# Handing out weight buffers and chaining the first loads at the beginning of an MLP

## The chip, the cores and the metric

The kernel runs on one core of a Trainium2 chip. Its time is the device time of one execution in microseconds (us); where several executions were timed, the median stands with the lowest and the highest. A core has TensorE for matrix products (PE in the profile), VectorE (DVE), ScalarE (ACT), GpSimd (POOL) and SyncE (SP). Each runs its own instructions in the order of its own queue, and they wait for each other by semaphores. DMAs are issued by SP and by POOL here and run beside the engines.

## The reference, cut to what matters

The kernel computes two layers of a decoder trunk on a sequence of 512 tokens, width 1024, in float32. Each layer is a mixer (attention and an mLSTM branch, merged and projected), and then the MLP at whose beginning the change lies:

```python
    x = x + mixed @ w_out

    u = jax.nn.relu(rmsnorm(x, norm_ffn) @ w_ff1)
    return x + (u * u) @ w_ff2
```

`w_ff1` is 1024 x 4096 and `w_ff2` 4096 x 1024, for each layer.

## The kernel before, in words

Every float32 product is made of three TensorE products: both factors are split into a high part, which ACT rounds, and a low part, the difference, which DVE forms. `two_parts` does that (lines 1212 and 1213), and `mm3` (line 47 stands for its matmuls) multiplies high by high, high by low and low by high.

The MLP is cut into four parts of 1024 hidden columns. In each part the first product (512 tokens x 1024 by 1024 x 1024) and the second one are done as 2 x 2 blocks with seven block products instead of eight, numbered 1 to 7, each on a sum or a difference of blocks. One block product is a slot; `first_slots` gives those of the first product of a part (`f0`, `f1` for the parts 0 and 1), `second_slots` those of the second one (`p`). A slot has two halves `h`, each with a weight tile of 512 KB (128 x 1024 float32). A half of a first slot is 24 matmuls with 256 columns moving, a half of a second slot 12 matmuls with 512 columns.

The list `slots` is the order of the work: f0[2], f1[2], f0[1], f0[5], p[1], f0[6], f0[7], f0[4], f0[3], f1[1] and so on. For each half the kernel first prepares (`prep`: ask for the weights, split them, then call `then`, which can ask for more) and later runs it; preparing is four halves ahead in the program. The pool `spl` holds four pairs of split weights, so the fifth split waits until TensorE is done with the first pair.

The weights lie in eleven raw buffers, numbered 0 to 10. `raw` (line 1227) hands out the first free number of the list `idle_raws`, and `drop` gives a number back at the end of the list, once the tile's splits are in the program. The buffers lie over memory that the mixer before has used, in four groups: 0 and 1 ("b"), 2 ("d"), 4 to 6 ("c"), and 3 and 7 to 10 ("a"); a group comes free when the mixer's last reader of that memory is done. `ask` (line 1236) issues a load on SP (line 1239); each of the first loads is ordered behind the one before it, and from the fifth on the scheduler places them as it likes.

What a slot needs, with the names of the tiles in the instruction order of layer 0 (of which the last number stays from here on):

- f0[2]: block (0,1) of part 0, loads 3703 and 3709. f1[2]: block (0,1) of part 1, loads 3715 and then, for the second half, 3727.
- f0[1]: block (0,0), loads 3779 and 3830.
- f0[5], f0[6], f0[3]: the sum blocks `s`. `begin` (line 1389 for part 0) loads a block into `c` (3721, 3733), another into `s` (3723, 3735), adds them on DVE (`plus`, line 1249) and lets POOL add a third block to `c` by an accumulating DMA (`more`, line 1348). After f0[5] has split `s`, POOL adds one more block to it for f0[6], and then another for f0[3].
- f0[7]: the blocks `c`. p[1]: blocks of `w_ff2`, loads 3958 and 3992. f0[4]: block (1,1), loads 4138 and 4173. The sum blocks of part 1: loads 4144 and 4179, each with an accumulating DMA behind it.

`begin0` is called in the prep of f1[2], so the sum blocks of part 0 take their buffers between the two halves of f1[2]; `begin1` is called in the prep of f0[4].

Beside the first five halves run the steps of the norm: for each of four column blocks `turn_whole` transposes x on TensorE into a bank of a pool of two (line 52), makes a high part on ACT (line 180) and a low part on DVE (line 181) for f0[1], and two scaled copies on ACT (line 1298). `t1` forms their difference on DVE, which ACT and DVE then split; it is the moving operand of f0[5]. `t2` does the same for f0[6]. After slot f0[2] ACT copies its bank to SBUF (line 1445), and so after f1[2], f0[5] and f0[6]; f0[7] adds to the bank that the copy after f0[6] reads.

Of the kernel before, what the change touches and what calls it, by code (L numbers as in the profile page):

```python
# [33 lines left out]
def hybrid_kernel(ctx, tc, x, norm_mix, w_in, att_q_norm, att_k_norm, att_sinks, m_gate_bias,  # L34
# [27 lines left out]
    def nm(s):  # L62
        uid[0] += 1
        return f"{s}_{uid[0]}"
# [4 lines left out]
    def pool(phase, name, bufs):  # L69
        now[name] = phase.enter_context(tc.tile_pool(name=name, bufs=bufs, reuse_waits="tile"))  # L70
        return now[name]
# [1114 lines left out]
    def mlp(l, norm, phase):  # L1186
# [6 lines left out]
        comb = pool(phase, "comb", 1)  # L1193
        uspl = pool(phase, "uspl", 2)
        spl = pool(phase, "spl", 4)
        raws, idle_raws = {}, list(range(11))
        for which, tags in (("a", (3, 7, 8, 9, 10)), ("b", (0, 1)), ("c", (4, 5, 6)), ("d", (2,))):
            raws.update(dict.fromkeys(tags, pool(phase, "raws_" + which, 1)))
        acts, ms = norm.acts, []
# [27 lines left out]
        def raw(shape):  # L1227

            n = idle_raws.pop(0)
            r = raws[n].tile(list(shape), F32, tag=f"r{n}", name=nm("raw"))  # L1230
            raw_place[id(r)] = (n, r)
            return r

        first_asked = []

        def ask(r, src):

            with tc.issue_after(first_asked[-1].ins) if first_asked else ExitStack():
                d = nc.sync.dma_start(r, src)  # L1239
            if len(first_asked) < 4:  # L1240
                first_asked.append(d)

        def drop(*gone):
# [3 lines left out]
        def plus(d, p, q, op=ALU.add):  # L1247
            with tc.high_priority():
                ve.tensor_tensor(d, p, q, op=op)
# [76 lines left out]
            t_parts[4] = two_parts(d, *t_new("t4"))  # L1326
            drop(d)

        def first_slots(part, new, places={}, begins=()):

# [2 lines left out]
            a11, a12, a22, s, c = ([None] * 2 for _ in range(5))  # L1335

            def src(h, i, j):
                c0 = 1024 * part + T * i + H * h
                return w_ff1[l, T * j:T * (j + 1), c0:c0 + H].rearrange("(k p) n -> p k n", p=P)

            def load(to, h, i, j):
                with tc.high_priority():
                    to[h] = raw([P, 4, H])
                    ask(to[h], src(h, i, j))

            def more(to, h, i, j):
                with tc.high_priority():
                    gp.dma_start(to[h], src(h, i, j), accum_op=ALU.add)  # L1348

            def w2(h):  # L1350
                load(a12, h, 0, 1)
                return a12[h], lambda: [f(h) for f in begins], a12[h]

            def begin(h):
                load(s, h, 1, 0)
                more(s, h, 1, 1)

            def w1(h):
                load(a11, h, 0, 0)
                return a11[h], lambda: begin(h) if part > 1 else None, a11[h]  # L1360

            def w5(h):
                def then():
                    more(s, h, 0, 0)
                    load(c, h, 0, 0)
                    more(c, h, 1, 0)

                return s[h], then
# [9 lines left out]

            def w4(h):
                load(a22, h, 1, 1)  # L1380
                return a22[h], lambda: [f(h) for f in begins] if part == 0 else None, a22[h]

            if part == 0:

                def begin(h):
                    load(c, h, 1, 0)
                    load(s, h, 1, 1)
                    plus(s[h], s[h], c[h])
                    more(c, h, 0, 0)

                def w2(h):
                    load(a12, h, 0, 1)
                    return a12[h], lambda: None, a12[h]

                def w5(h):
                    return s[h], lambda: more(s, h, 0, 0)
# [74 lines left out]
            else:  # L1471
                done1, done2 = lambda: then_read((0, 0), False, ALU.add), lambda: first_read((0, 0), True)

            return begin, {
                1: product_(1, False, True, w1, lambda: quad(0, 0), done1),
                2: product_(2, True, not seeded, w2, lambda: quad(1, 0), done2),
                5: product_(5, True, True, w5, lambda: t_parts[1], lambda: first_read((1, 1), True, -1.0)),
                6: product_(6, False, False, w6, lambda: t_parts[2], lambda: first_read((1, 0), False)),
                7: product_(7, False, False, w7, lambda: t_parts[3], lambda: then_read((1, 1), False, ALU.subtract)),
                4: product_(4, False, False, w4, lambda: t_parts[4], lambda: only_read((0, 1), False, -1.0)),  # L1480
                3: product_(3, True, False, w3, lambda: quad(1, 1), lambda: then_read((1, 0), True, ALU.add)),
            }
# [40 lines left out]
        def second_slots(part, u):  # L1523
# [9 lines left out]
            def load(to, h, i, j):  # L1533
                with tc.high_priority():
                    to[h] = raw([P, 2, T])
                    ask(to[h], src(h, i, j))
# [83 lines left out]


        us = [{key: quads.tile([P, 4, H], F32, tag=t, name=nm("u")) for key, t in buf[0].items()}, {}, {}, {}]
        f1s = []
        begin0, f0 = first_slots(0, us[0], {2: "y", 5: "y"}, [lambda h: f1s[0](h)])
        begin1, f1 = first_slots(1, us[1], {2: "x"}, [begin0])
        f1s.append(begin1)
        p = second_slots(0, us[0])
        slots = [f0[2], f1[2], f0[1], f0[5], p[1], f0[6], f0[7], f0[4], f0[3],
                 f1[1], p[5], f1[5], p[6], f1[6], p[3], f1[7], p[7], f1[3], p[4], f1[4], p[2]]
        for part in range(1, 4):  # L1630
            p = second_slots(part, us[part])
            if part < 3:
                f = first_slots(part + 1, us[part + 1])[1]
                slots += [p[1], f[1], p[2], f[2], p[5], f[5], p[6], f[6], p[3], f[7], p[7], f[3], p[4], f[4]]
            else:
                slots += [p[n] for n in (1, 5, 2, 6, 3, 7, 4)]
# [46 lines left out]
    for l in range(DEPTH):  # L1683
        with start if l == 0 else ExitStack() as phase:
            if l > 0:
                psum_pools(phase, 3)
            norm = mixer(l, norm, late, order, phase)
        with ExitStack() as phase:
            psum_pools(phase, 2)
            norm = mlp(l, norm, phase)  # L1690
        late = norm.steps(0, 1.5, 0.5, lambda k, norm=norm: turn_behind(norm, k)) if norm else []
        order = [4, 5, 6, 7, 0, 1, 2, 3]
# [40 lines left out]
```

## Time and profile before

| | |
|---|---|
| three timed executions | median 1309.32 us (1307.10 to 1311.42) |
| the profiled execution's own time | 1310.44 us |
| its span, from the first to the last instruction | 1308.7 us |
| TensorE busy | 1268.4 us, 97% |
| beginning of the MLP of layer 0, 322 to 337 us | TensorE busy for 6.71 of 15.00 us |
| mean granted clock of TensorE | 0.990 |

The profile shows one execution. In its groups and timelines a row has the engine, the line, the operation, what is written from what (without buffer numbers), the shape, the count and, in brackets, how long the engine stood idle before it and which work ended that. Times in a timeline are us from the start of the span. The lines of the timelines that matter are shown with the prediction.

### The profile page before, as it was taken

How to read it: one execution, taken by the hardware profiler on the slowest of the kernel's cores; microseconds unless marked ns; L12 is line 12 of the kernel's file. 1: busy time of each engine (PE TensorE's matmuls, PEld its weight loads, DVE VectorE, ACT ScalarE, POOL GpSimd, SP SyncE). 2: the span in 40 equal slices, each digit the busy share in tenths (PEclk: the TensorE clock that was granted, in tenths of full speed). 3: DMA queues.
4: the chain of work that ended last, by engine and by line, in shares of the span. 5: the costliest groups of instructions: out<-in, count | busy, mean ns of one | idle time of the engine just before them, and what ended most of it. 6: DMA issues, size and time to landing. Idle time of an engine off the chain costs nothing.

```text
span 1308.7 us, 19864 instructions
## 1 busy us (share of the span) xinstructions
PE 1268.4 (97%) x7170; PEld 1106.3 (85%) x7170; DVE 1027.8 (79%) x1620; ACT 818.1 (63%) x1435; POOL 289.2 (22%) x377
## 2 busy tenths in 40 slices
PE   9999999999699999999999999999996999999998
PEld 7887888888588989999888887888876988999987
DVE  5788987687668886878857989876876688778787
ACT  6578587645656665656554885875465556566563
POOL 4514131030213012131215132310303130211300
PEclk9999999999899999999999999999997999999999
DMA  5425463485998879897224345545859997899953
GB/s 158 114 68 150 106 114 113 133 163 147 193 228 150 224 184 212 218 192 210 34 72 113 108 112 114 111 121 128 170 155 190 227 170 206 185 210 228 193 145 97
DMA packets 147379, 201.78 MB, mean 154 GB/s; under 512 B 10825, under 2 KB 87473, under 8 KB 147281
## 3 DMA queue, kind: packets, MB, share of 16 engines
q0 software_dynamic: 52544, 70.39, 33.6%
q1 hardware_dynamic: 94016, 129.72, 32.5%
q8 instruction: 56, 0.92, 0.3%
q10 hardware_dynamic: 720, 0.40, 0.1%
q14 instruction: 43, 0.34, 0.1%
HBM read 197.33 MB, written 2.10 MB: 152 GB/s over the span
## 4 chain that ended last, share of the span: by engine, by line
PE 82%; DVE 6%; DMA 4%; ACT 3%; issue 2%; POOL 1%; SPq 0%; DVEq 0%; ACTq 0%; POOLq 0%
PE mm L47 70%; PE aux L47 11%; DMA raw<-in_w_ff_dram 4%; DVE wl L1213 2%; PE aux L52 2%; ACT t L664 1%; ACT wh L1212 1%; DMA w<-in_w_in_dram 1%; DVE wl L168 1%; DVE tq L625 0%; DVE p L748 0%; SPq L1239 0%; ACT u L1445 0%; POOL rp L547 0%; POOL rq L548 0%
## 5 line engine op out<-in xcount | busy, mean ns | idle before, releaser
L1213 DVE TENSOR_TENSOR wl<-raw,wh 128x1024 fp32r<-128x1024 f32 x224 | 270.9, 1220 | 118.5 <-ACT wh L1212 117.5
L47 PE MATMUL mm<-i,wh 128*128 128x256 f32 (+1 forms) x1344 | 336.8, 342 | 22.0 <-ACT wh L1212 18.1
L1212 ACT ACTIVATE wh<-raw 128x1024 fp32r<-128x1024 f32 x224 | 235.0, 1054 | 179.1 <-PE mm L47 88.7
L47 PEld LDWEIGHTS mm<-i,wh 128*128 128x128 f32 x1344 | 227.5, 193 | 43.0 <-ACT wh L1212 19.1
L47 PE MATMUL mm<-i,wl 128*128 128x256 f32 (+1 forms) x672 | 225.7, 337 | 0.0
L47 PE MATMUL mm<-wh,uh 128*128 128x512 f32 x440 | 172.7, 392 | 0.2 <-ACT uh L1212 0.2
L47 PE MATMUL mm<-wl,uh 128*128 128x512 f32 x440 | 172.1, 391 | 0.0
L47 PE MATMUL mm<-wh,ul 128*128 128x512 f32 x440 | 171.5, 390 | 0.0
L1348 POOL DMA_DIRECT2D raw<-in_w_ff_dram x60 | 77.5, 1315 | 407.0 <-DVE wl L1213 114.8
L47 PEld LDWEIGHTS mm<-i,wl 128*128 128x128 f32 x672 | 129.0, 192 | 13.4
L168 DVE TENSOR_TENSOR wl<-w,wh 128x512 fp32r<-128x512 f32 (+1 forms) x144 | 96.4, 673 | 37.2 <-ACT wh L167 36.2
L167 ACT ACTIVATE wh<-w 128x512 fp32r<-128x512 f32 (+1 forms) x144 | 86.4, 603 | 62.4 <-PE mm L47 43.9
L47 PE MATMUL mm<-t,wh 128*128 128x256 f32 x576 | 106.6, 287 | 5.9 <-ACT wh L1212 5.9
L47 PE MATMUL mm<-wh,i 128*128 128x512 f32 (+1 forms) x352 | 99.7, 357 | 1.5 <-ACT i L180 1.0
L47 PEld LDWEIGHTS mm<-t,wh 128*128 128x128 f32 x576 | 92.2, 195 | 7.7 <-ACT wh L1212 6.3
L47 PEld LDWEIGHTS mm<-wh,ul 128*128 128x128 f32 x440 | 82.8, 188 | 17.4
L47 PEld LDWEIGHTS mm<-wh,uh 128*128 128x128 f32 x440 | 83.0, 189 | 16.5 <-ACT uh L1212 0.6
L47 PEld LDWEIGHTS mm<-wl,uh 128*128 128x128 f32 x440 | 83.0, 189 | 15.7
L47 PE MATMUL mm<-t,wl 128*128 128x256 f32 x288 | 82.6, 287 | 1.5 <-DVE wl L1213 1.5
L1540 POOL DMA_DIRECT2D raw<-in_w_ff_dram x40 | 50.4, 1341 | 149.1 <-DVE wl L1213 98.9
L1267 DVE SCALAR_TENSOR_TENSOR x<-mm,ms,x 128x512 f32<-128x512 f32 x102 | 72.3, 744 | 8.7 <-PE mm L47 8.4
L47 PEld LDWEIGHTS mm<-wh,i 128*128 128x128 f32 x352 | 61.9, 188 | 10.9 <-ACT i L180 1.2
(323 smaller groups left out, 2535.5 us busy)
## 6 DMA issues: line engine op xcount, KB each, us to landing
raw<-in_w_ff_dram SPq DMA_DIRECT2D x144, 512.0 KB, 5.5
raw<-in_w_ff_dram POOLq DMA_DIRECT2D x100, 512.0 KB, 8.5
w<-in_w_in_dram SPq DMA_DIRECT2D x112, 256.0 KB, 2.7
a<-in_w_in_dram POOLq DMA_DIRECT2D x32, 256.0 KB, 5.9
qa<-in_w_out_dram POOLq DMA_DIRECT2D x12, 512.0 KB, 5.9
a<-in_w_in_dram SPq DMA_DIRECT2D x16, 256.0 KB, 4.1
w<-in_w_att_branch_dram SPq DMA_DIRECT2D x16, 256.0 KB, 2.8
w<-in_w_m_branch_dram SPq DMA_DIRECT2D x16, 256.0 KB, 2.8
```

The lines of the kernel that those rows point to most:

```text
L47: latest[0] = nc.tensor.matmul(*args, **kw)
L52: latest[0] = nc.tensor.transpose(*args)
L167: sc.activation(wh[:, :off], raw[:, :off], AF.Copy)
L168: ve.tensor_tensor(wl[:, :off], raw[:, :off], f32(wh[:, :off]), op=ALU.subtract)
L664: sc.activation(s3[:, i, :], s3[:, i, :], AF.Exp, bias=m[:, i:i + 1], accum_out=den[:, i:i + 1])
L1212: sc.activation(hi, src, AF.Copy)
L1213: ve.tensor_tensor(lo, src, f32(hi), op=ALU.subtract)
L1267: ve.scalar_tensor_tensor(xh[:, cc], ps[i][:, cc], ms[j][:, b:b + 1], xh[:, cc], op0=ALU.mult, op1=ALU.add)
L1348: gp.dma_start(to[h], src(h, i, j), accum_op=ALU.add)
L1540: gp.dma_start(to[h], src(h, i, j), accum_op=ALU.add)
```

## The change

Three things change, all in `mlp`, and so in both layers.

- `idle_raws` starts as 0, 1, 2, 9, 8, 7, 10, 3, 4, 5, 6 instead of 0 to 10.
- Each of the first ten loads is ordered behind the one before it, instead of the first four.
- `begin0` is no longer called in the prep of f1[2], but in that of f0[1], behind its own load. `begin1` stays in the prep of f0[4], written without the lists of functions.

```diff
-        raws, idle_raws = {}, list(range(11))
+        raws, idle_raws = {}, [0, 1, 2, 9, 8, 7, 10, 3, 4, 5, 6]
...
-            if len(first_asked) < 4:
+            if len(first_asked) < 10:
                 first_asked.append(d)
...
-        def first_slots(part, new, places={}, begins=()):
+        def first_slots(part, new, places={}, behind=None):
...
             def w2(h):
                 load(a12, h, 0, 1)
-                return a12[h], lambda: [f(h) for f in begins], a12[h]
+                return a12[h], lambda: None, a12[h]
...
             def w1(h):
                 load(a11, h, 0, 0)
-                return a11[h], lambda: begin(h) if part > 1 else None, a11[h]
+                return a11[h], lambda: begin(h) if part != 1 else None, a11[h]
...
             def w4(h):
                 load(a22, h, 1, 1)
-                return a22[h], lambda: [f(h) for f in begins] if part == 0 else None, a22[h]
+                return a22[h], lambda: behind and behind(h), a22[h]
...
-
-                def w2(h):
-                    load(a12, h, 0, 1)
-                    return a12[h], lambda: None, a12[h]
...
-        f1s = []
-        begin0, f0 = first_slots(0, us[0], {2: "y", 5: "y"}, [lambda h: f1s[0](h)])
-        begin1, f1 = first_slots(1, us[1], {2: "x"}, [begin0])
-        f1s.append(begin1)
+        begin1, f1 = first_slots(1, us[1], {2: "x"})
+        f0 = first_slots(0, us[0], {2: "y", 5: "y"}, begin1)[1]
```

On SP, at the beginning of the MLP of layer 0, these loads stood in a row before, from the first of a sum block on. By the names above: c for h 0 (3721), s (3723), c for h 1 (3733), p[1] (3958), f0[4] (4138), f0[1] for h 1 (3830), p[1] for h 1 (3992), f0[1] for h 0 (3779), f1[2] for h 1 (3727), s for h 1 (3735).

```order
L1239 DMA raw_802_3721<-in_w_ff1_dram 128x4x256
L1239 DMA raw_803_3723<-in_w_ff1_dram 128x4x256
L1239 DMA raw_807_3733<-in_w_ff1_dram 128x4x256
L1239 DMA raw_842_3958<-in_w_ff2_dram 128x2x512
L1239 DMA raw_865_4138<-in_w_ff1_dram 128x4x256
L1239 DMA raw_822_3830<-in_w_ff1_dram 128x4x256
L1239 DMA raw_845_3992<-in_w_ff2_dram 128x2x512
L1239 DMA raw_816_3779<-in_w_ff1_dram 128x4x256
L1239 DMA raw_804_3727<-in_w_ff1_dram 128x4x256
L1239 DMA raw_808_3735<-in_w_ff1_dram 128x4x256
```

The load for the second half of f1[2] is the ninth of this row and stands behind that for f0[4], the eighth slot.

The same place on SP now. The numbers are dealt anew: f1[2] for h 1 is 3721 here, f0[1] is 3767 and 3824, c is 3773 and 3830, s is 3775 and 3832; p[1], f0[4] and the sum blocks of part 1 keep theirs.

```order
L1239 DMA raw_802_3721<-in_w_ff1_dram 128x4x256
L1239 DMA raw_812_3767<-in_w_ff1_dram 128x4x256
L1239 DMA raw_815_3773<-in_w_ff1_dram 128x4x256
L1239 DMA raw_816_3775<-in_w_ff1_dram 128x4x256
L1239 DMA raw_820_3824<-in_w_ff1_dram 128x4x256
L1239 DMA raw_823_3830<-in_w_ff1_dram 128x4x256
L1239 DMA raw_824_3832<-in_w_ff1_dram 128x4x256
L1239 DMA raw_842_3958<-in_w_ff2_dram 128x2x512
L1239 DMA raw_865_4138<-in_w_ff1_dram 128x4x256
L1239 DMA raw_873_4179<-in_w_ff1_dram 128x4x256
L1239 DMA raw_870_4173<-in_w_ff1_dram 128x4x256
L1239 DMA raw_868_4144<-in_w_ff1_dram 128x4x256
```

The load for f1[2] moved from the ninth place to the first, f0[1] and the sum blocks follow in the order of use, and what comes late now is p[1] for h 1 (3992), which is the next row after these.

On ACT, this is what stood before between the last two scaled copies of the norm's steps and the copy of the bank of f1[2]. 3906 is the difference that `t1` splits, and 3729 and 3781 are the high parts for f1[2] and f0[1].

```order
L1298 ACTIVATE x_814_3775<-aux_826_3861,gcol_85 128x256
L1298 ACTIVATE x_815_3776<-aux_826_3861,gcol_85 128x256
L262 ACTIVATE junk_86,nss_691_3147<-x1_0_89 128x512 x2
L1212 ACTIVATE wh_805_3729<-raw_804_3727 128x1024
L1212 ACTIVATE wh_817_3781<-raw_816_3779 128x1024
L1212 ACTIVATE t1_831_3908<-raw_830_3906 128x1024
L1212 ACTIVATE wh_823_3832<-raw_822_3830 128x1024
L1212 ACTIVATE wh_827_3874<-raw_803_3723 128x1024
```

And this is what stands on ACT now, from the split of the second sum block (3832) to that of `t1`.

```order
L1212 ACTIVATE wh_839_3928<-raw_824_3832 128x1024
L1441 ACTIVATE u_829_3903<-mm_825_3836 128x512 x2
L1298 ACTIVATE x_810_3763<-aux_819_3815,gcol_85 128x256
L1298 ACTIVATE x_811_3764<-aux_819_3815,gcol_85 128x256
L1298 ACTIVATE x_810_3763<-aux_826_3861,gcol_85 128x256
L1298 ACTIVATE x_811_3764<-aux_826_3861,gcol_85 128x256
L1212 ACTIVATE wh_843_3960<-raw_842_3958 128x1024
L262 ACTIVATE junk_86,nss_691_3147<-x0_0_87 128x512
L1212 ACTIVATE t1_831_3908<-raw_830_3906 128x1024
```

The weight splits moved ahead of the norm's copies, and the four copies of the last two turns, with `t1` behind them, moved behind the copy of the bank of f1[2].

## The prediction

> **What bounds the kernel now.** I read the page first: TensorE is busy nearly throughout, and of its 40 slices two stand out.
>
> ```profile
> PE 1268.4 (97%) x7170; PEld 1106.3 (85%) x7170; DVE 1027.8 (79%) x1620; ACT 818.1 (63%) x1435; POOL 289.2 (22%) x377
> PE   9999999999699999999999999999996999999998
> ```
>
> A slice is 32.7 us, so the two sixes begin at 327 and 982 us: the beginnings of the two MLPs. A gain elsewhere would have to shorten TensorE's work, which the change leaves alone. So I went to TensorE's timeline there, layer 0 first.
>
> ```profile
> 327.41 0.40 PE L47 MATMUL mm<-i,wh 128*128 128x256 f32 x2
> 327.77 0.40 PE L47 MATMUL mm<-i,wh 128*128 128x256 f32 x2
> ...
> 328.13 0.62 PE L52 MATMUL aux<-ident,x 128*128 128x128 f32 x4
> 338.07 0.80 PE L47 MATMUL mm<-i,wh 128*128 128x256 f32 x2 [9.31 <-ACT wh L1212]
> ...
> 340.46 0.63 PE L47 MATMUL mm<-i,wh 128*128 128x256 f32 x2
> 341.10 0.63 PE L47 MATMUL mm<-i,wh 128*128 128x256 f32 x2
> ...
> 358.02 0.50 PE L47 MATMUL mm<-t,wh 128*128 128x256 f32 x2 [2.69 <-ACT wh L1212]
> 359.27 0.39 PE L47 MATMUL mm<-t,wl 128*128 128x256 f32 x1 [0.76 <-DVE wl L1213]
> ...
> 361.00 0.63 PE L47 MATMUL mm<-t,wh 128*128 128x256 f32 x2
> 361.64 0.63 PE L47 MATMUL mm<-t,wh 128*128 128x256 f32 x2
> ...
> 364.27 0.39 PE L47 MATMUL mm<-wh,uh 128*128 128x512 f32 x1
> 364.50 0.40 PE L47 MATMUL mm<-wl,uh 128*128 128x512 f32 x1
> ...
> 374.43 0.51 PE L47 MATMUL mm<-i,wh 128*128 128x256 f32 x2 [1.94 <-ACT u L1445]
> ```
>
> In a bracket stand the idle time and what ended it. The wait of 9.31 us is for the second half of f1[2]; those of 2.69 and 0.76 us are for f0[6]; the last one, before f0[7], is for the copy of a bank. The starts also show the clock: three matmuls take 0.36 us at 327 us, but 0.64 us after the long wait and again after the second one.
>
> Both weight waits end with ACT's split, and ACT was itself waiting for a DMA:
>
> ```profile
> 336.96 2.00 ACT L1212 ACTIVATE wh<-raw 128x1024 fp32r<-128x1024 f32 x2 [4.03 <-DMA raw<-in_w_ff_dram]
> ...
> 356.91 1.06 ACT L1212 ACTIVATE wh<-raw 128x1024 fp32r<-128x1024 f32 x1 [4.99 <-DMA raw<-in_w_ff_dram]
> ```
>
> SP's timeline shows when the loads were asked for (start, length, count), and the view of the DMAs how long they took from issue to landing: one alone (issued at 306.08), the six from 322.19, then an accumulating one beside the six (323.92), one in traffic (346.38) and one alone (398.14).
>
> ```profile
> 306.08 0.37 SPq L1239 DMA_DIRECT2D raw<-in_w_ff_dram  x1
> 311.66 0.37 SPq L1239 DMA_DIRECT2D raw<-in_w_ff_dram  x1
> 322.19 3.51 SPq L1239 DMA_DIRECT2D raw<-in_w_ff_dram  x6
> 339.30 4.91 SPq L1239 DMA_DIRECT2D raw<-in_w_ff_dram  x3
> ```
>
> ```profile
> raw<-in_w_ff_dram SPq DMA_DIRECT2D x1, 512.0 KB, 3.6
> raw<-in_w_ff_dram SPq DMA_DIRECT2D x6, 512.0 KB, 8.4
> raw<-in_w_ff_dram POOLq DMA_DIRECT2D x1, 512.0 KB, 12.2
> raw<-in_w_ff_dram POOLq DMA_DIRECT2D x1, 512.0 KB, 10.4
> raw<-in_w_ff_dram POOLq DMA_DIRECT2D x1, 512.0 KB, 6.3
> ```
>
> By SP's order the load that f1[2] lacks is the fifth of the six: SP sat until 322.19 before the load for f0[4], whose buffer was still being split, and everything behind it waited. Its own buffer's group had been free since 311.66, when its neighbour in that group (s, buffer 4) was asked for. The row at 339.30 holds the loads for part 1's sum blocks; the last of its three goes out near 344.
>
> **What is there to win.** From the end of the transposes (328.13 + 0.62 = 328.75) to 374.43 are 45.7 us. The work in it: seven halves of 24 matmuls (the second of f1[2], two each of f0[1], f0[5], f0[6]) at eight times 0.36 = 2.88 us, 20.2 us; and p[1], 24 matmuls at 364.50 - 364.27 = 0.23 us, 5.5 us. Together 25.7 us. So 20.0 us are waits and half clock, of which the 1.94 us before f0[7] stay, since it adds to a bank that ACT must have read: 18.0 us could go. Layer 1:
>
> ```profile
> 978.29 0.62 PE L52 MATMUL aux<-ident,x 128*128 128x128 f32 x4
> 987.37 0.80 PE L47 MATMUL mm<-i,wh 128*128 128x256 f32 x2 [8.45 <-ACT wh L1212]
> ...
> 1023.57 0.51 PE L47 MATMUL mm<-i,wh 128*128 128x256 f32 x2 [1.94 <-ACT u L1445]
> ```
>
> From 978.91 to 1023.57, less 25.7 and 1.94, leaves 17.0 us. The change can win 35.0 us at most.
>
> **The change, part by part.** *Buffers and chain.* The load for f1[2] now takes the place and the group of buffers of the load issued at 306.08, and behind it go four more of the same group (f0[1], c, s, f0[1]); c and s for h 1 follow at about 311.7. Six loads landed in 8.4 us as the median, so five in a row from 306 are there by about 317, and of these the first, for f1[2], is there ten us before TensorE can use it. The wait of 9.31 us goes, and the half clock behind it. The load alone costs nothing; what hides the five is that the 16 engines have room there (last column but one, their share); the mixer has no loads left. The view is the busy times by stretches:
>
> ```profile
> 306.00:312.00 6.00, 6.00 (x34) 4.95 (x33) 5.46 (x9) 2.52 (x4) 0.00 (x0) 1.00 0.28 87
> ...
> 322.00:337.00 15.00, 6.71 (x55) 6.27 (x54) 5.67 (x9) 9.13 (x23) 1.30 (x1) 0.87 0.89 240
> ...
> 345.00:355.00 10.00, 10.00 (x86) 10.00 (x85) 8.05 (x8) 5.96 (x8) 2.28 (x3) 1.00 1.19 223
> ```
>
> *What is late next, first:* t1. ACT's new order puts two weight splits ahead of copies of the norm that free the banks for the last transposes; these may then start some tenths late, 0.5 us (0 to 1). Behind the end of f1[2], ACT runs a split, the two copies of the bank and four scaled copies, then DVE the difference, ACT a split and DVE its low part:
>
> ```profile
> 324.72 1.09 ACT L1445 ACTIVATE u<-mm 128x512 f32<-128x512 f32 x2
> 327.20 1.57 ACT L1298 ACTIVATE x<-aux,gcol 128x256 f32<-128x256 f32 x4 [0.24 <-DVE i L181]
> ```
>
> ```profile
> L1213 DVE TENSOR_TENSOR wl<-raw,wh 128x1024 fp32r<-128x1024 f32 x224 | 270.9, 1220 | 118.5 <-ACT wh L1212 117.5
> L1212 ACT ACTIVATE wh<-raw 128x1024 fp32r<-128x1024 f32 x224 | 235.0, 1054 | 179.1 <-PE mm L47 88.7
> ```
>
> That is 1.05 + 1.09 + 1.57 + 1.22 + 1.05 + 1.22 = 7.2 us, and 0.5 for what ACT has in between and the hops; f0[1] covers 2 x 2.88 = 5.76. So f0[5] waits 1.9 us (0 to 4: four if each hop and each split ahead is as late as can be).
>
> *Sum blocks later.* They land by about 318, so nothing waits for their loads. The accumulating DMA that f0[6] needs comes behind f0[5]'s split of s. That split is the seventh, so it waits for TensorE to end the first half of f1[2], some 328.4 us; ACT and DVE are through with it at about 332, POOL issues at about 332.7 instead of 346.38:
>
> ```profile
> 346.38 1.29 POOL L1348 DMA_DIRECT2D raw<-in_w_ff_dram  x1 [1.52 <-DVE wl L1213]
> 354.01 2.62 POOL L1348 DMA_DIRECT2D raw<-in_w_ff_dram  x2 [6.34 <-issue]
> ```
>
> With 10.4 us, as in that traffic, it lands at 343.1; the ends are 339 (6.3) and 345 (12.2). The traffic stays: four loads (f0[4] and part 1, then p[1]) go out on SP at about 329, when the buffers of f0[1] are split. TensorE reaches f0[6] at 328.8 + 0.5 + 2.88 + 5.76 + 1.9 + 5.76 = 345.6. Then ACT's split (1.05) and on DVE two low parts (2.4), s and t2, follow the landing and what ACT has queued: a wait of 3.0 us, 1.7 if the block is early, 5 if late.
>
> *Clock.* After 2.69 + 0.76 us of waiting the triples took 0.64 us until shortly before 364.27, over some 3.4 us; 0.28 of each 0.64 is loss, 1.5 us. The waits that I expect (1.9, then 3.0) are of that size; I count it once per layer. [...]
>
> *The rest* (`behind`, `places`) only moves text; f0[4]'s and part 1's loads have 20 us of other slots ahead of them.
>
> **The sum.** New waits per layer 0.5 + 1.9 + 3.0 + 1.5 = 6.9 us. Gain 18.0 - 6.9 = 11.1 in layer 0, 17.0 - 6.9 = 10.1 in layer 1, 21.2 us. From the profiled execution's 1310.44 that is 1289.2; the three timed ones have their median 1.1 us lower, so **1288.0 us**. At their ends the new waits are 1.7 + 0 to 1 + 4 + 5 + 3: gains of 31.6 down to 9.0 us, or 1278 to 1300.
>
> **The rivals.**
>
> *The DMA engines are the limit.* What is asked for earlier then only queues: in the stretch from 345 us their share is 1.19. [...] Then the accumulating DMAs land as late after their issue as bytes allow, and only the five loads that move into the free stretch are won: of the six that took from 322.19 to 336.96, 14.8 us, five sixths, 12.3 us, less the new waits of 5.4 us: 6.9 per layer, 1310.4 - 13.8 - 1.1 = 1296 us. Against it: the share of 0.28 from 306 us on, room that it now uses.
>
> *Slower: POOL's queue holds up f0[6].* The second accumulate of s for h 1 stands on POOL behind that of a block of part 1, which must have been loaded; before, POOL sat 6.34 us for this, issued two at 354.01, and ACT split the second, s for h 1, at 363.66:
>
> ```profile
> 363.66 1.06 ACT L1212 ACTIVATE wh<-raw 128x1024 fp32r<-128x1024 f32 x1 [3.65 <-DMA raw<-in_w_ff_dram]
> ```
>
> TensorE's order now has all of f0[6]'s first half and two matmuls of the second ahead of most of p[1]; it gets there at about 351.5. If the load is as late as it was, TensorE waits till 365.5 for the splits, 14 us instead of none: 11.1 - 14 = 3 us lost per layer, 1310.4 + 6 - 1.1 = 1315 us. It decides from a landing at about 361 on. Against it: the load goes out at about 329, not near 344.
>
> *Nothing changes.* If the new group's buffer is not free at 306 but with the mixer's very end, f1[2] waits as before: 1309 us. Against it: that group is the one asked for at 306.08.
>
> **Chances.** Faster and slower mean by over 0.3%, 3.9 us, about what a measurement of this kernel can tell from no change. My forecast 0.68; DMA limit 0.20; slower 0.07; nothing 0.05. So faster 0.88, same 0.05, slower 0.07. The range goes from 1278 to 1302: it holds the forecast's bounds and the DMA limit's case, this also with two stretches of half clock per layer (1296 + 2 x 3.0), and leaves out the other two rivals and some of the tails.
>
> **What would show it.** Right: SP's second row at 306 becomes five; the wait of 9.31 us is gone in both layers, and no 0.64 us triples follow; f0[5] waits 1 to 3 us for t1, f0[6] 2 to 5 us; f0[7] starts near 363 instead of 374.43, and near 1002 instead of 1023.57 once layer 0's gain is counted too. Wrong: a wait over 5 us before f0[5] or f0[6]; POOL idle for several us ahead of the accumulates; or a wait of several us past f0[7].

## The result, and the profile after

The changed kernel takes 1293.25 us (median of four executions, 1289.04 to 1297.91), the kernel before 1309.65 us (median of four, 1307.10 to 1311.42). The ratio is 0.9877 with a 95% interval of 0.9836 to 0.9918: faster, by 16.4 us. The forecast was 1288.0 us, in a range of 1278 to 1302. The profiled execution of the changed kernel is the shortest of the four, 1289.04 us with a span of 1287.3 us, so the other three lie above what this profile shows; a second profile is used beside it below.

On the page, the two sixes in TensorE's row of slices have become eights:

```profile
PE 1263.0 (98%) x7170; PEld 1103.0 (86%) x7170; DVE 1026.8 (80%) x1620; ACT 817.3 (63%) x1435; POOL 282.7 (22%) x377
PE   9999999999899999999999999999998999999998
```

SP's timeline has five loads in a row from 303.35 us (one before), two more at 309.93, and, behind two single ones, a row of four at 326.97:

```profile
303.35 2.97 SPq L1239 DMA_DIRECT2D raw<-in_w_ff_dram  x5
309.93 0.92 SPq L1239 DMA_DIRECT2D raw<-in_w_ff_dram  x2
...
326.97 2.83 SPq L1239 DMA_DIRECT2D raw<-in_w_ff_dram  x4
```

TensorE's timeline, layer 0 and then layer 1. In brackets stand the idle time and what ended it:

```profile
337.16 0.39 PE L47 MATMUL mm<-t,wh 128*128 128x256 f32 x1 [0.87 <-DVE t L1213]
...
345.53 0.58 PE L47 MATMUL mm<-t,wh 128*128 128x256 f32 x1 [2.47 <-ACT wh L1212]
348.00 0.58 PE L47 MATMUL mm<-t,wh 128*128 128x256 f32 x1 [1.88 <-DVE t L1213]
...
363.21 0.51 PE L47 MATMUL mm<-i,wh 128*128 128x256 f32 x2 [1.94 <-ACT u L1441]
...
984.99 0.38 PE L47 MATMUL mm<-t,wh 128*128 128x256 f32 x1 [2.97 <-ACT wh L1212]
987.46 0.58 PE L47 MATMUL mm<-t,wh 128*128 128x256 f32 x1 [2.08 <-DVE t L1213]
...
1002.15 0.51 PE L47 MATMUL mm<-i,wh 128*128 128x256 f32 x2 [1.94 <-ACT u L1441]
```

The waits of 9.31 and 8.45 us for f1[2] are gone. What is late now is t1 before f0[5] (0.87 us) and, before f0[6], first the split of `s` and then `t2` (2.47 and 1.88 us; 2.97 and 2.08 in layer 1). f0[7] starts at 363.21 and 1002.15 us, where the forecast had "near 363" and "near 1002"; how much of that is luck stands below.

How much of this is the change's own shows when the same 330 matmuls, those that end at the start of f0[7], are measured in both kernels. In the busy times by stretches the second column is the length and the third TensorE's busy time; of before:

```profile
308.00:374.43 66.43, 51.37 (x333) 46.83 (x331) 46.11 (x55) 41.14 (x65) 12.81 (x10) 0.90 0.86 189
958.17:1023.57 65.40, 50.89 (x332) 46.40 (x330) 45.20 (x53) 41.14 (x65) 12.82 (x10) 0.90 0.84 184
```

of the profiled execution of the changed kernel:

```profile
306.27:363.21 56.94, 49.74 (x333) 45.34 (x331) 45.17 (x52) 40.59 (x65) 12.80 (x10) 0.94 0.96 222
945.24:1002.15 56.91, 49.00 (x333) 44.69 (x331) 46.32 (x54) 40.58 (x65) 12.81 (x10) 0.97 0.99 227
```

The stretches are 9.5 and 8.5 us shorter, 18.0 us together, while the spans differ by 1308.7 - 1287.3 = 21.4 us. The other 3.4 us lie outside these stretches, 1.7 us before the first and 1.7 us between the two, and a second profiled execution doesn't have them in sum (run e12 below).

### The profile page after: what moved, and what is told of

Read it like the earlier page. It is cut to its first block, busy times and chain, and to the rows that moved or that the text cites. A ratio compares the mean times of both kernels' runs of the same rounds, so it can differ in the third digit from the quotient of the medians.

```text
span 1287.3 us, 19870 instructions
## 1 busy us (share of the span) xinstructions
PE 1263.0 (98%) x7170; PEld 1103.0 (86%) x7170; DVE 1026.8 (80%) x1620; ACT 817.3 (63%) x1435; POOL 282.7 (22%) x377
## 4 chain that ended last, share of the span: by engine, by line
PE 92%; DVE 2%; DMA 2%; ACT 2%; issue 1%; SPq 0%; DVEq 0%; POOL 0%; ACTq 0%; POOLq 0%
PE mm L47 78%; PE aux L47 12%; PE aux L52 2%; DMA raw<-in_w_ff_dram 2%; DVE wl L1213 1%; ACT wh L1212 1%; ACT u L1441 0%; SPq L1239 0%; DVE x L1267 0%; DMA w<-in_w_in_dram 0%; DVE u L1249 0%; DVE t L1213 0%; DVE s L1249 0%; ACT u L1455 0%; DVE u L1454 0%
## 5 line engine op out<-in xcount | busy, mean ns | idle before, releaser
L47 PE MATMUL mm<-i,wh 128*128 128x256 f32 (+1 forms) x1344 | 333.4, 339 | 4.0 <-ACT u L1441 3.9
L47 PEld LDWEIGHTS mm<-i,wh 128*128 128x128 f32 x1344 | 224.4, 190 | 24.6 <-ACT u L1441 4.3
L47 PEld LDWEIGHTS mm<-wl,uh 128*128 128x128 f32 x440 | 83.1, 189 | 15.5
```

The lines of the kernel that those rows point to most:

```text
L47: latest[0] = nc.tensor.matmul(*args, **kw)
```

## The experiments

Four theories were tried, in two pairs. That *the place in SP's row decides* when f1[2] can go on, against *the group of buffers decides* (runs e1 to e3). Then, on the wait before f0[6] that came out larger than forecast: *theory A*, that ACT stands still for p[1]'s late load and everything behind it on ACT is late, against *theory B*, that the accumulating DMA into `s` lands late (e4 to e10).

ACT's timeline of the changed kernel had suggested A:

```profile
340.97 1.06 ACT L1212 ACTIVATE wh<-raw 128x1024 fp32r<-128x1024 f32 x1 [3.76 <-DMA raw<-in_w_ff_dram]
...
343.50 1.04 ACT L1212 ACTIVATE t<-raw 128x1024 fp32r<-128x1024 f32 x1
344.44 1.04 ACT L1212 ACTIVATE wh<-raw 128x1024 fp32r<-128x1024 f32 x1
```

The first row is the split of p[1]'s second load (3992), the other two are t2 and the split of `s`, h 0, for f0[6].

**e1, the list alone.** The kernel before with the new list:

```diff
-        raws, idle_raws = {}, list(range(11))
+        raws, idle_raws = {}, [0, 1, 2, 9, 8, 7, 10, 3, 4, 5, 6]
```

> Only the order of the buffers is changed. Theory (the place in SP's row decides): the load for the second half of f1[2] still stands ninth, behind that for f0[4], so it goes out at about 324 us as before, the wait of 9 us stays in both layers, and the time is 1307 to 1312 us. Rival (the group of buffers decides): a buffer that the mixer frees at 306 us instead of 311.7 brings the load forward, the wait shrinks by some 5 us per layer, and the time is near 1299 us.

1310.65 us beside 1309.06 for the kernel before, ratio 1.001 (0.9994 to 1.0026). TensorE's long wait is still there:

```profile
337.64 0.79 PE L47 MATMUL mm<-i,wh 128*128 128x256 f32 x2 [9.92 <-ACT wh L1212]
```

So a buffer that is free earlier is worth nothing while its load stands behind f0[4]'s.

**e2, the chain alone.** The kernel before with the longer chain:

```diff
-            if len(first_asked) < 4:
+            if len(first_asked) < 10:
```

> Only the chain is longer, ten loads instead of four; buffers and sum blocks as before. Theory (the place in SP's row decides): the load for the second half of f1[2] goes out third of a row at about 312 us, lands by 318 and its wait is gone; f0[1] stands further back but goes out by 317 too; so it has nearly the whole gain, 1291 to 1299 us. Rival (the three parts are worth a third each, or the group of buffers decides): at most 7 us of gain, 1302 us or more.

1285.85 us, ratio 0.9814 (0.9787 to 0.984): not only nearly the whole gain but more than all three parts together bring, 5 us beyond the expected range. The long wait is gone. TensorE now waits for the last high part that the norm's steps make, because ACT has it behind a split that waits for TensorE to give a pair of split weights back (0.68 us) and behind three copies:

```profile
333.80 0.38 PE L47 MATMUL mm<-i,wh 128*128 128x256 f32 x1 [1.93 <-ACT i L180]
334.58 0.42 PE L47 MATMUL mm<-i,wh 128*128 128x256 f32 x1 [0.40 <-DVE i L181]
```

```profile
330.77 1.06 ACT L1212 ACTIVATE wh<-raw 128x1024 fp32r<-128x1024 f32 x1 [0.68 <-PE mm L47]
331.74 1.06 ACT L1445 ACTIVATE u<-mm 128x512 f32<-128x512 f32 x2
332.69 0.48 ACT L1298 ACTIVATE x<-aux,gcol 128x256 f32<-128x256 f32 x1
333.05 0.70 ACT L180 ACTIVATE i<-aux,gcol 128x512 fp32r<-128x512 f32 x1
```

Before f0[6] it waits for no weights at all. But TensorE's order has moved as well: it runs p[1] behind the first matmul of f0[6] and goes on with f0[6] only at 353.06 us.

**e3, the sum blocks alone.** The third part of the change by itself; list and chain as before.

```diff
             def w2(h):
                 load(a12, h, 0, 1)
-                return a12[h], lambda: [f(h) for f in begins], a12[h]
+                return a12[h], lambda: None, a12[h]
...
-                return a11[h], lambda: begin(h) if part > 1 else None, a11[h]
+                return a11[h], lambda: begin(h) if part != 1 else None, a11[h]
```

> Only the sum blocks are asked for later; list and chain as before. The second half of f1[2] now has the fourth place of the chain and goes out at about 306 to 312 us, so its wait is gone, but the second half of f0[1] stands eleven places further back on SP, behind the loads for f0[4], p[1] and a sum block of part 1, which wait for buffers. Theory (the place in SP's row decides): the wait moves to f0[1] or f0[5], 5 to 12 us per layer in place of 9, and the time is 1300 to 1315 us. Rival (it is enough that f1[2] is early, since what comes behind it has slack): 1290 to 1298 us.

1295.66 us, ratio 0.9888 (0.9863 to 0.9914). The wait did move to the second half of f0[1], with smaller ones before f0[6], 6.9 us in layer 0. The time is 4 us below the expected range, in which I had left the waits before f0[6] as they were: 2.69 + 0.76 us before and 1.00 + 0.76 here in layer 0, 3.18 + 0.76 and 1.10 + 0.76 in layer 1.

```profile
338.11 0.80 PE L47 MATMUL mm<-i,wh 128*128 128x256 f32 x2 [4.73 <-ACT wh L1212]
340.23 0.58 PE L47 MATMUL mm<-i,wl 128*128 128x256 f32 x1 [0.37 <-DVE wl L1213]
351.52 0.51 PE L47 MATMUL mm<-t,wh 128*128 128x256 f32 x2 [1.00 <-ACT wh L1212]
352.78 0.39 PE L47 MATMUL mm<-t,wl 128*128 128x256 f32 x1 [0.76 <-DVE wl L1213]
```

Together, e1 to e3 settle the first question: the place in SP's row decides. Two of the three parts move f1[2]'s load forward in that row, each alone, and end its wait; the list alone does not.

**e4, a chain of twelve** in the changed kernel, so that p[1]'s load for h 1 stands ahead of f0[4]'s:

```diff
-            if len(first_asked) < 10:
+            if len(first_asked) < 12:
```

> The changed kernel with a chain of twelve loads: p[1]'s load for h 1 stands behind p[1]'s for h 0 on SP, ahead of f0[4] and of part 1's blocks. Theory A (in the changed kernel ACT's split of that load, late at 341 us, holds back the work behind it on ACT, among it t2 and the split for f0[6]): the load goes out near 320 us instead of 329.3, ACT's wait of 3.8 us goes, f0[6] waits under 2 us instead of 2.47 + 1.88, half clock shrinks, and the time is 3 to 10 us below the changed kernel's. Theory B (the accumulating DMA for f0[6] lands late, near 344 us, and sets the wait alone): 2 us or more of wait stay and the time is within 2 us of the changed kernel's.

1280.80 us, ratio 0.9778 (0.9753 to 0.9804). The wait before f0[6] is 0.97 us in place of 2.47 + 1.88, and the profile's mean granted clock is 1.000. It came out as theory A had it, but SP's timeline shows that more had moved than p[1]'s load: four loads go out from 320.14 on and one at 327.80, where the changed kernel has one at 320.46 and four from 326.97. SP no longer stands before a load of part 1's sum blocks (4179) with the others behind it. So A and B were not told apart.

```profile
320.14 4.33 SPq L1239 DMA_DIRECT2D raw<-in_w_ff_dram  x4
327.80 0.37 SPq L1239 DMA_DIRECT2D raw<-in_w_ff_dram  x1
```

**e5, p[1] splits another tile.** This one tells them apart. All DMAs stay, but ACT need not wait for p[1]'s second load, since it splits a tile of the norm in its place (p[1]'s second half is so computed with other numbers):

```diff
                 if part == 0:
-                    return qa[h], lambda: more(qa, h, 0, 1)
+                    r = whole[0].rearrange("p (a c) n -> p a (c n)", a=2) if h else qa[h]
+                    return r, lambda: more(qa, h, 0, 1)
```

> The changed kernel, but p[1]'s second half splits a tile of the norm that has long been there instead of its own weights (so this half is multiplied by other numbers); the load of these weights and every other DMA stay in their order. Theory A (ACT, standing still from 337.2 to 341.0 us for that load, holds back t2 and the split behind it): the accumulating DMA for f0[6] still lands at 341 to 343 us, but TensorE's wait before f0[6] falls from 2.47 + 1.88 us to under 1.5 us in both layers, and the time is 3 to 10 us below the changed kernel's, 1283 to 1290. Theory B (the landing sets the wait): f0[6] still waits 2 us or more, and the time is 1291 to 1296 us.

1290.66 us, ratio 0.9862 (0.9844 to 0.9879), 0.3 us under the range that B had. ACT's wait for p[1]'s load is gone and t2 is split at 340.19 instead of 343.50, but then ACT waits for the accumulating DMA, and TensorE waits 1.66 + 2.08 us, not much less than the 2.47 + 1.88 of the changed kernel:

```profile
340.19 1.04 ACT L1212 ACTIVATE t<-raw 128x1024 fp32r<-128x1024 f32 x1
344.17 1.06 ACT L1212 ACTIVATE wh<-raw 128x1024 fp32r<-128x1024 f32 x1 [2.94 <-DMA raw<-in_w_ff_dram]
```

```profile
345.28 0.39 PE L47 MATMUL mm<-t,wh 128*128 128x256 f32 x1 [1.66 <-ACT wh L1212]
347.74 0.58 PE L47 MATMUL mm<-t,wh 128*128 128x256 f32 x1 [2.08 <-DVE t L1213]
```

Theory A falls: what ACT waited for was only the first of two late transfers. The second wait even grew, 2.08 us against 1.88: DVE makes t2's low part (from 346.47 us) only behind the low part of `s` (from 345.26).

**e9, the DMAs into `c` behind those into `s`** (run after the next three, but it closes this question). SP's loads stay; only POOL's order changes:

```diff
                     plus(s[h], s[h], c[h])
-                    more(c, h, 0, 0)
 
                 def w5(h):
-                    return s[h], lambda: more(s, h, 0, 0)
+                    def then():
+                        with tc.issue_after(more(s, h, 0, 0).ins):
+                            more(c, h, 0, 0)
+
+                    return s[h], then
```

> The changed kernel, but POOL issues the accumulating DMAs into the blocks c behind those into the blocks s; SP's loads stay in their order. Theory B (the landing of the accumulating DMA into s, h 0, sets the wait before f0[6], and it lands late because two accumulating DMAs of 2.65 us each stand before it): it lands some 5 us earlier, TensorE's wait before f0[6] falls from 2.47 + 1.88 us to under 1.5 us in both layers, and the time is 3 to 10 us below the changed kernel's, 1283 to 1290. Rival (ACT's wait for p[1]'s load, or ACT's row itself, sets it): 2 us or more stay, 1291 to 1296 us.

1284.49 us, ratio 0.9802 (0.9778 to 0.9826), 7.4 us below the changed kernel on the same chip (e12). In the view of the DMAs (KB of one, us from issue to landing) the accumulating DMA into `s`, h 0, which POOL issues at 330.17 in the changed kernel, takes

```profile
raw<-in_w_ff_dram POOLq DMA_DIRECT2D x1, 512.0 KB, 13.5
```

and here, issued at 331.40 with none before it on POOL,

```profile
raw<-in_w_ff_dram POOLq DMA_DIRECT2D x1, 512.0 KB, 8.9
```

so it is there at 340.3 us instead of 343.7. The wait before f0[6] falls to 0.95 us, nearly that of e4 (0.97). A new one of 1.00 us stands before its second half, so in sum 1.95 us are left, more than the expected 1.5:

```profile
345.37 0.39 PE L47 MATMUL mm<-t,wh 128*128 128x256 f32 x1 [0.95 <-DVE t L1213]
349.84 0.51 PE L47 MATMUL mm<-t,wh 128*128 128x256 f32 x2 [1.00 <-ACT wh L1212]
```

Theory B holds: in the changed kernel the wait is set by what shares the engines with that DMA. e4 had done the same from the other side: there the blocks of `c` still stand first, but the loads are gone earlier, and the DMA, issued at 331.00, takes 9.6 us.

**e6, the changed kernel without the new list:**

```diff
-        raws, idle_raws = {}, [0, 1, 2, 9, 8, 7, 10, 3, 4, 5, 6]
+        raws, idle_raws = {}, list(range(11))
```

> The changed kernel with the old order of the buffers (0 to 10). Theory A: p[1]'s load for h 1 still stands behind all of part 1's loads on SP, so ACT waits for it as in the changed kernel; the first loads go out at 311 instead of 306 us, which costs f1[2] at most 2 us: 1291 to 1298 us. Rival (the list is what costs the changed kernel 7 us against the chain alone): 1284 to 1288 us.

1294.03 us, ratio 0.9892 (0.9875 to 0.991), as the changed kernel. Before f0[6] it waits 2.46 and 2.08 us. The time agrees with theory A, but by e5 the reason is B's: the loads of part 1 stay where they are. With e1 this makes two kernels in which the list brings nothing that can be measured.

**e7, the changed kernel with the sum blocks asked for as before**, that is e3's diff taken back:

```diff
-                return a12[h], lambda: None, a12[h]
+                return a12[h], lambda: [f(h) for f in begins], a12[h]
...
-                return a11[h], lambda: begin(h) if part != 1 else None, a11[h]
+                return a11[h], lambda: begin(h) if part > 1 else None, a11[h]
```

> The changed kernel with the sum blocks asked for in the prep of f1[2], as before. On SP p[1]'s load for h 1 then stands two places further ahead, third behind f0[4]'s first. Theory A: ACT gets it at about 335 us, no wait at f0[6] over 1.5 us, and f1[2]'s load goes out at 305 to 307 us, so no wait there: 1279 to 1286 us. Rival (asking for the sum blocks later is part of the gain): 1293 us or more.

1285.84 us, ratio 0.9826 (0.9812 to 0.9841), at the end of the expected range. No wait for weights is left before f0[6], but one of 1.93 + 0.40 us stands where I expected none: it is that of e2, for the norm's last high part. So the later sum blocks are what costs the changed kernel 6 to 7 us against its own other parts (1293.25 and, in e12, 1291.87).

How they cost it is not only a matter of DMAs. The accumulating DMA into `s`, h 0, lands hardly earlier here (issued at 331.82, 11.1 us, so at 342.9 against 343.7), and t2's low part is done no earlier (348.3 us against 347.9). What differs is TensorE: it comes to f0[6] at 346.50 in place of 343.06, and its order, as in e2, puts p[1] behind the first matmul of f0[6], so that it goes on with f0[6] only at 352.22. The changed kernel has f0[6]'s first half ahead of most of p[1].

```profile
346.50 0.34 PE L47 MATMUL mm<-t,wh 128*128 128x256 f32 x1
...
352.22 0.28 PE L47 MATMUL mm<-t,wh 128*128 128x256 f32 x1
```

No run moved the order of TensorE alone, so what it is worth by itself stays open.

**e8, the same with a chain of twelve**, e7's and e4's edits together.

> New buffer order, sum blocks as before, chain of twelve: f1[2]'s load goes out at 305 to 307 us and p[1]'s load for h 1 at about 320. Theory A: with both loads early no wait over 1.5 us is left ahead of f0[7] in either layer, and the time is 1277 to 1283 us, within 3 us of the changed kernel with a chain of twelve. Rival (f0[6]'s accumulating DMA, asked for no earlier, becomes the late one): 1284 us or more.

1285.24 us, ratio 0.9824 (0.9807 to 0.984). The number is the rival's, the mechanism isn't: the DMA into `s` lands at 340.9 us, TensorE, in e7's order, goes on with f0[6] behind the first matmul only at 352.61, and apart from the 1.94 us before f0[7] the largest wait is the one of e2 and e7:

```profile
333.39 0.38 PE L47 MATMUL mm<-i,wh 128*128 128x256 f32 x1 [1.93 <-ACT i L180]
```

**e10, e9's order of the accumulating DMAs with e4's chain**, both diffs together.

> The same with a chain of twelve loads. Theory B: its profile with the old order of c has a wait of only 0.97 us before f0[6], so at most 1 us per layer is left to win: 1277 to 1281 us. Rival (c's blocks, now later, become late for f0[7]): slower than with the chain of twelve alone, 1283 us or more.

1279.95 us (1278.88 to 1280.92), ratio 0.9766 (0.9743 to 0.9788), as theory B had it.

**e11, the chain of twelve once more**, on the chip of e9, e10 and e12.

> The changed kernel with a chain of twelve once more: 1279 to 1284 us, and 9 to 14 us below the changed kernel beside it on the same chip.

1280.47 us, ratio 0.9769 (0.9747 to 0.9792), 11.4 us below the changed kernel beside it. e10 and e11 can't be told apart; both beat the changed kernel and the kernel before.

**e12, the changed kernel once more**, with no edit.

> The changed kernel once more: 1289 to 1298 us. Theory (waits of about 2 us cost half clock only where they fall into one window of 3.41 us of a grid whose place differs from run to run): its profile shows the same waits as before within 1 us, but other stretches of half clock, each beginning a multiple of 3.413 us after the first, and a longer time where these are longer.

1291.87 us (1289.57 to 1294.94), ratio 0.9857 (0.9835 to 0.988). Its profile is that of the longest of the five, with a span of 1293.2 us. The stretches that end at f0[7]:

```profile
306.89:364.86 57.97, 50.16 (x333) 45.89 (x331) 45.19 (x52) 40.56 (x65) 12.81 (x10) 0.94 0.96 224
949.70:1008.08 58.38, 49.17 (x332) 44.79 (x330) 45.39 (x53) 40.45 (x65) 12.81 (x10) 0.94 0.95 221
```

Here the change gains 8.5 and 7.0 us, 15.5 together, and that is all by which the spans differ (1308.7 - 1293.2). The waits before f0[6] are 2.87 + 2.08 and 4.47 + 1.88 us, so the expected "within 1 us" failed in layer 1: 6.35 us in sum there against 5.05.

## Why the prediction was right, and where it was off

*The wait for f1[2] goes*: right, in both layers, and for the reason given (e1 to e3). The new order of the buffers has no part in it: the five loads from 306 us on were not needed, since e2, whose load for f1[2] goes out only after 310.8 us, has no wait for it either.

*What there is to win*: the forecast had 18.0 and 17.0 us. With a chain of twelve (e4) the same matmuls run at full clock throughout and are busy for 47.35 us:

```profile
307.10:358.27 51.17, 47.35 (x332) 43.36 (x330) 45.41 (x53) 40.51 (x65) 12.81 (x10) 1.00 1.04 237
```

So before lost 66.43 - 47.35 = 19.1 us and 65.40 - 47.35 = 18.1; less the 1.94 us that stay, 17.1 and 16.1 could be won. My count of the work was 0.9 us too low.

*The turn and t1*: 0.5 and 1.9 us were forecast, none and 0.87 measured; together 1.5 us too high.

*f0[6]*: the term that was mis-sized most. Forecast 3.0 us; measured 4.35 and 5.05 in one profile, 4.95 and 6.35 in the other. In layer 1 the two waits together go beyond the 5 us that the prediction itself named as a sign of being wrong, though no single wait does. The issue of the accumulating DMA was earlier than forecast (330.17, not 332.7), but it took 13.5 us where 10.4 had been carried over, and its end, 343.7, met a TensorE that was there 2.5 us earlier (343.06, not 345.6). The step that failed is "the traffic stays". This is what the DMA engines moved from its issue to its landing (packets, MB, share of the 16 engines), before (346.38 to 356.82 us) and then in the changed kernel (330.17 to 343.69), accumulating DMAs as q0 and plain loads as q1:

```profile
q0 software_dynamic: 1497, 1.48, 91.7%
q1 hardware_dynamic: 535, 0.53, 17.9%
```

```profile
q0 software_dynamic: 1411, 1.40, 64.8%
q1 hardware_dynamic: 1856, 2.10, 49.3%
```

The accumulating ones are no more than they were: before, too, others stood ahead on POOL. But four loads go beside it in place of one. The prediction names these four, and yet it takes over the time of a row that had one. At 1.3 us a load (last section) three more are 3.9 us, where 3.1 were measured. e4 and e9 show that neither side decides alone: with the loads gone it is 9.6 us, with the blocks of `c` behind it 8.9.

*Half clock*: 1.5 us per layer was forecast; the busy times less 47.35 give 2.4 and 1.7 us in one profile, 2.8 and 1.8 in the other. That waits of this size cost clock was right: with those of 2.47 + 1.88 us, which end at 345.53 and 348.00 us, the granted clock is 0.50 from 345.48 to 352.31 us (last section).

*The sum.* In layer 0 the new losses are 0.87 + 4.35 + 2.4 = 7.6 us against 6.9, and 17.1 - 7.6 = 9.5 is what the stretches show. Over both profiles the gain is 16.7 us as a mean ((18.0 + 15.5) / 2), not 21.2, and 1309.65 - 16.7 = 1292.95 is where the median lies. There is luck in how near this comes: the turn and t1 were 1.5 us too dear in layer 0, f0[6] and the half clock 2.2 us too cheap, so most of it cancels. And that f0[7] starts so near 363 and 1002 is luck too, since 1.7 us of the first and 3.4 of the second come from outside the stretches; e12 has it at 364.86 and 1008.08.

*The rivals.* That the DMA engines are the limit was given 1296 us. It has part of the truth: its price is nearer to the median than my forecast is, and the excess over the forecast sits in a DMA that queued. e4 and e9 show what it queued behind: the same DMA is ready 3 us earlier (at 340.6 and 340.3 us against 343.7) when loads of SP, or accumulating DMAs of POOL, are moved out of its way. But it is the order that counts: with all bytes kept, 11 us go (e11 against e12). That POOL's queue holds up f0[6] by a load was wrong, and that nothing changes too.

## What to carry to other kernels

Look first at the order in which one queue issues its loads: a load that waits for its buffer holds up all that stand behind it (in e1 TensorE waits 9.92 us for one of these), and a buffer that is free earlier helps none of them. When a transfer is pulled forward, ask what it now stands before, and put the one that is needed first ahead in its queue (here an accumulating DMA into `s` before those into `c`). Look whether the order of the other engines has moved with it: in e2 and e7 it was TensorE's. And an experiment that comes out as one theory says has not shown it as long as the edit moved the rival's cause as well.

## What the runs showed of the hardware

**The accumulating DMAs moved half as many bytes as the loads in the same time.** The view of the DMAs for 342 to 344 us of the changed kernel, when only accumulating ones were under way (packets, MB, share of the 16 engines), and for 364 to 366, when only plain loads were:

```profile
q0 software_dynamic: 396, 0.39, 124.6%
```

```profile
q1 hardware_dynamic: 589, 0.79, 106.9%
```

With the engines full both times (shares of 124.6% and 106.9%), 0.39 MB go in 2 us against 0.79. The size of the packets is not the reason: 208 of these loads' 589 are of 2 KB or more, but from 308 to 311.5 us, where all are under 2 KB, as they are in the accumulating DMAs, plain loads move 1.34 MB in 3.5 us (383 GB/s against 196):

```profile
q1 hardware_dynamic: 1355, 1.34, 108.6%
```

At these rates, as an estimate, a block of 512 KB is 2.7 us of all engines as an accumulating DMA (0.52 MB at 196 GB/s) and 1.3 us as a load (at 397 GB/s, of the 0.79 MB). Whether the adding costs it, or that POOL issues it, is not shown: no plain load of a block is issued by POOL in these kernels. From issue to landing of the DMA into `s` the engines moved 0.71 MB of accumulating DMAs and 1.54 MB of loads in e9, in place of 1.40 and 2.10 in the changed kernel; by these prices that is 3.5 + 1.4 us less, and 4.6 were measured. Of the two blocks of `c` it is chiefly the second that e9 takes out of the way, since the first landed 1.1 us after `s` was issued (issued at 325.13, it took 6.1 us).

**Half clock came in steps of 3.41 us, also behind steps in which TensorE was busy for 1.48 us.** In the profiles of before, of the changed kernel and of e12, the stretches with a granted clock of 0.50 begin and end (but for the end of the run) on one grid of 3.413 us per execution. Before they run from 333.10 to 343.34, 360.41 to 363.82, 981.64 to 991.88 and 1008.94 to 1012.36 us, that is from 0 to 3, 8 to 9, 190 to 193 and 198 to 199 steps from the first; in the changed kernel from 345.48 to 352.31 and 987.19 to 990.60, from 0 to 2 and 188 to 189; in e12 they begin at 348.00, 365.07 and 989.71 us, 0, 5.0 and 188.0 steps from the first. Four windows of e9, of the busy times by stretches (length, TensorE busy, and the clock third from the end):

```profile
354.56:357.97 3.41, 3.41 (x26) 3.11 (x24) 2.65 (x7) 1.12 (x2) 0.00 (x0) 1.00 1.11 215
357.97:361.39 3.42, 1.48 (x13) 1.46 (x13) 2.33 (x4) 1.91 (x2) 0.00 (x0) 1.00 1.16 237
361.39:364.80 3.41, 3.41 (x18) 3.41 (x18) 0.00 (x0) 0.00 (x0) 0.00 (x0) 0.50 1.16 274
364.80:368.21 3.41, 3.41 (x30) 3.41 (x30) 1.97 (x2) 1.06 (x1) 0.00 (x0) 1.00 1.15 262
```

The wait of 1.94 us before f0[7] falls wholly into the second window, which is busy for 1.48 us, and the next one runs at a granted clock of 0.50. In the changed kernel the same wait is cut by the grid, and the clock stays at 1.00:

```profile
359.14:362.55 3.41, 2.13 (x18) 1.92 (x17) 2.78 (x4) 1.96 (x3) 0.00 (x0) 1.00 1.15 279
362.55:365.96 3.41, 2.75 (x23) 2.75 (x24) 1.03 (x2) 0.61 (x1) 0.00 (x0) 1.00 1.07 398
```

The grid lies differently in the two profiles of the changed kernel: the first of these stretches begins at 345.48 us in one and at 348.00 in the other, 0.74 steps later. So the same wait can cost 1.7 us more in one than in the next, as an estimate from one step of 3.41 us at a clock of 0.50; by this it is part of why the changed kernel's times spread over 9 us and those of e10, whose profile has a mean granted clock of 1.000, over 2. The shortest of the four has a granted clock of 0.996 and the longest one of 0.993; as an estimate from these, 0.004 x 1287 and 0.007 x 1296 us are lost, 5 and 9, so some 4 of the 9 us are clock. What the clock goes by is not shown. Behind two windows that were busy for 1.48 us of 3.41 (e9, from 357.97, and before, from 357.00) it was 0.50; a window busy for 1.75 us (before, from 353.58) kept the clock, and one busy for 1.97 us (e3, from 993.08) lost it, so the busy time as the profile models it does not decide alone.
